# A decoder layer on one core: attention's filling passes as one sequence, and four output tiles begun early

## The chip, the cores and the metric

The kernel runs on 1 core of a Trainium2 chip. The metric is the device time of one execution in microseconds (us), as the median of several runs. Engines are named as in the profile: PE is the matrix engine (PEld its weight loads), DVE the vector engine, ACT the scalar engine, POOL the general engine, SP the engine that issues most DMAs.

## The reference, cut to what matters

One decoder layer over 1024 tokens of width 1024, in float32:

```python
h = rms_norm(x, norm_mix_pre)
q_d, k_d, v_d, u_p, q_m, gate_logits = split(h @ w_in)
a = diff_attention(q_d, k_d, v_d, lam)       # 8 heads, two softmax maps each, ALiBi, causal
a = rms_norm(a, subln_g) * (1 - lam_init)    # per head
y_attn = a @ w_attn_branch
y_pool = multiscale_pool(u_p, pool_w, pool_scale) @ w_pool_branch
y_mem  = memory_cross_attention(q_m, rms_norm(mem), w_mem_kv) @ w_mem_branch
gates = sigmoid(gate_logits)                 # three gates of width 1024
mix = gates[0]*y_attn + gates[1]*y_pool + gates[2]*y_mem
x = x + rms_norm(mix @ w_out, norm_mix_post)
h2 = rms_norm(x, norm_ffn_pre)
g, v = split(causal_depthwise_conv3(h2 @ w_up))
x = x + rms_norm((gelu(g) * v) @ w_down, norm_ffn_post)
```

## The kernel before, in words

Each float32 factor is kept as a high and a low part, and a product is three matrix passes (`mm3`, lines 103 to 105 of the profile). `split` (lines 89 and 90) makes the parts: ACT copies the high one, DVE subtracts for the low one. Products are made for 128 output channels by 512 tokens, over 8 blocks `k` of 128 input channels: 24 passes for such a half, 48 for both.

The parts of the layer run one after another: norms and the memory branch, the pooling branch, the two branches' gates and mix (`mixp_d`), values, keys and queries, attention, the merge of the attention branch, the output projection, the channel mixer. Many results are written to memory and read back.

Attention goes through 8 heads, each with 4 blocks `b` of two query tiles `u`. In a head, `scores` makes two maps of scores on PE (`pss`, line 1176), adds the bias and takes the extremum on DVE (`z`, line 1180), and takes exponentials on ACT (line 1185); `combine` joins the two maps on DVE (line 1199); `turn_weights` transposes them on PE (`pta`, line 1215) and splits them (`aT`); `weigh_values` multiplies by the values (`poa`, line 1232); `head_norm` sums squares on PE (`pn`, line 1250). The weights of a block are turned during the next block, so the last block of a head is finished in the first block of the next.

Between these stages `weave` puts filling: products that attention doesn't wait for at once. A generator is cut into steps by its `yield`s, and `steps(gen, n)` gives n closures that advance it. The filling of the kernel before is

- `head_keys(h + 1)` in heads 1 to 6: the keys of the next head but heads 0 and 1 (`pqk`), in 4 steps of 12 passes. Their weights were split earlier and lie in memory (`wk_d`). A half's result is split into `ktmp` and copied by four DMAs into the head's key tiles `ks` (line 1125). There are two sets of key tiles, for even and for odd heads;
- `gate(dt)`: the logits of gate 0 for 128 channels (`pg`), 8 steps of 6 passes. Its weights are loaded and split by `wsplit` at once. ACT copies a half out (`g`, line 1145), and POOL stores it to `gate_d`. Gates 0 and 1 were made ahead and wait in `g01` for their store;
- `values(h + 1)`: two loads of the next head's values, without passes.

Which head has which gate is a table:

```python
GATES = ((2, 3), (), (), (), (), (), (), (4,))
```

Weights of both kinds lie in the tags `wh` and `wl` of the pool `wst`, two buffers each; raw weights in `raw`, two buffers; `ktmp`, `g` and the tiles of the merge in the tag `t` of `gq`, two buffers. The banks of the matrix results are two of `b1`, two of `pj`, and two pairs of `b2`.

The order of instructions on each engine is not the order of the program text alone: a planner walks through the program with a model of times and lets an instruction go ahead of earlier ones that it takes to be not ready. So passes of gates can run before the place where they stand in the text. `issue_after` holds an instruction behind another one on its engine. On the chip each engine then runs its list in order.

Behind attention, gates 5 to 7 follow. Meanwhile the norms of heads 4 to 7 are finished (`head_norms(1)`, whose result `r_d` goes through memory), and each head's result `a` is loaded with its norm `rb`, scaled on DVE (line 1399) and split into `ath`, `atl`. The merge multiplies by `w_attn_branch` for 8 output tiles `dt` (`pya`): `merge_heads(dt, g)` does heads 0 to 3 (g = 0) or 4 to 7 (g = 1). Tiles 0 and 1 begin with heads 0 to 3 while heads 4 to 7 are not ready. `merge` loads the gate and `mixp_d` (`gm`, lines 1424 and 1425), takes the sigmoid on ACT (line 1426), multiplies and adds on DVE (lines 1427 and 1428) and splits into `mixh`, `mixl`. Then the output projection begins (`pout`).

Of the kernel before, what the change touches and what calls it, by code (L numbers as in the profile page):

```python
# [15 lines left out]
P = 128  # L16
# [6 lines left out]
NH = 8  # L23
# [18 lines left out]
def kernel(  # L42
# [1051 lines left out]
    def key_tiles(h):  # L1094
        return [qkp.tile([P, S], F32R, tag="ks%d%d" % (c, h % 2), name="ks%d" % c) for c in range(2)]
# [8 lines left out]

    def head_keys(h):


        wh, wl = [wst.tile([P, KT, P], F32R, tag=t, name=t) for t in ("wh", "wl")]
        with tc.issue_after(last["keys"].ins):
            for e, w in enumerate((wh, wl)):  # L1110
                nc.sync.dma_start(out=w.bitcast(F32), in_=wk_d[h, :, e])
        ks = key_tiles(h)
        for i in range(2):
            hs = slice(i * H, (i + 1) * H)
            pq = pbank(name="pqk")
            for k in range(KT):
                if k == H4:
                    yield
                mm3(pq, wh[:, k, :], wl[:, k, :], hTh[i][:, k, :], hTl[i][:, k, :], k == 0, k == KT - 1)
            tmp = gq.tile([P, 2, H], F32R, tag="t", name="ktmp")  # L1120
            split(tmp[:, 0, :], tmp[:, 1, :], pq)
            for c in range(2):
                for e in range(2):
                    r = 64 * (c ^ e)
                    nc.sync.dma_start(out=ks[c][r:r + 64, hs].bitcast(F32),
                                      in_=tmp[c * 64:c * 64 + 64, e, :].bitcast(F32))
            if i == 1:
                kts[h] = ks
            yield
# [170 lines left out]
    last["keys"] = last["load"]  # L1300
    with tc.issue_after(last["load"].ins):
        ready[3] = wsplit(chunk(w_in, C_G + 3 * P), [P, KT, P])
        for dt in range(2):
            nc.sync.dma_start(out=gate_d[dt], in_=g01[dt])
    GATES = ((2, 3), (), (), (), (), (), (), (4,))
    blocks = [(h, b) for h in range(NH) for b in range(4)]
    for h in range(NH):
# [34 lines left out]
        fillers = []  # L1342
        if h + 1 < NH:
            if h:
                fillers += steps(head_keys(h + 1), 4)
            for n, step in enumerate(steps(values(h + 1), 2)):
                fillers.insert(2 * n + 1, step)
        n = 0
        for dt in GATES[h]:
            for step in steps(first if dt == 2 else gate(dt), 6 if dt == 2 else 8):  # L1350
                fillers.insert(min(n, len(fillers)), step)
                n += 2
# [18 lines left out]
    def merge_heads(dt, g):  # L1371

        if g == 0:
            pys[dt] = wsplit(chunk(w_attn_branch, dt * P), [P, KT, P])[:2] + (bank(name="pya"), pbank(name="pya"))
        wh, wl, *py = pys[dt]
        for i in range(2):
            hs = slice(i * H, (i + 1) * H)
            for k in range(g * HG, (g + 1) * HG):
                mm3(py[i], wh[:, k, :], wl[:, k, :], ath[k][:, hs], atl[k][:, hs], k == 0, k == KT - 1)

    with tc.tile_pool(name="sub", reuse_waits="tile", bufs=4, side="right") as sub:
# [3 lines left out]
        for dt in range(5, KT):  # L1385
            for step in steps(gate(dt), 8):
                step()
        for h in range(NH):
            if h == HG:
                with tc.issue_after(ends["square"].ins):  # L1390
                    head_norms(1)

                for dt in range(2):
                    merge_heads(dt, 0)
# [23 lines left out]
    def merge(dt):  # L1418

        for i, py in enumerate(pys.pop(dt)[2:]):  # L1420
# [10 lines left out]
    for dt in range(KT):  # L1431
        if dt >= 2:
            merge_heads(dt, 0)
        merge_heads(dt, 1)
        merge(dt)
# [377 lines left out]
```

## Time and profile before

| what | value |
|---|---|
| median of 3 runs | 1727.56 us (1726.93 to 1729.04) |
| the profiled execution | 1727.11 us |
| its span, first to last instruction | 1725.3 us |
| granted clock of PE | 0.999 |
| head 0, heads 1 to 6, head 7 | 601.9, 638.3, 834.4 to 880.0 us of the span |
| gates behind attention | to 907.0 us |
| merge | 907.0 to 994.2 us |

A row of the timeline has the start, the time, the engine, the line, the operation, output and inputs, shapes, and in brackets the engine's idle time before it with what released it. A row of the table of waits has who waited for whom, the total, how often and the longest. A row by stretch has the stretch, its length, the busy time of each engine with its number of instructions, the granted clock, the share of the DMA engines and GB/s. The records of PE's passes overlap, and their ends are modelled.

### The profile page before, as it was taken

To read this page: it belongs to the slowest core of one execution; us is meant where nothing else is said; L and a number is where in the kernel's file an instruction comes from. 1 tells how busy PE (TensorE), PEld (TensorE's weight loads), DVE (VectorE), ACT (ScalarE), POOL (GpSimd) and SP (SyncE) were. 2 spreads that over 40 slices of the span, in tenths; PEclk is the share of its full clock that TensorE was granted. 3 is DMA by queue.
4 is the path that set the end of the run, shared out by engine and by line. 5 is a ranking of instruction groups with operands and counts; after the bars stand their busy time and mean duration, and the time that the engine had idled before them with its cause. 6 is when DMAs were issued, how large, how long until landed. Compare 5 with 4: busy or idle time off the path is not lost.

```text
span 1725.3 us, 22424 instructions
## 1 busy us (share of the span) xinstructions
PE 1711.3 (99%) x8106; PEld 1420.2 (82%) x8106; DVE 1242.2 (72%) x2059; ACT 888.5 (51%) x1585; POOL 45.0 (3%) x103
## 2 busy tenths in 40 slices
PE   9999999999999999999999999999999999999998
PEld 6888888888888888888888888888888888888886
DVE  7676876666666468888866555848888888877466
ACT  5434544444544467777744344645555555543453
POOL 0000000000000011111110000000000000000000
PEclk9999999999999999999999999999999999999999
DMA  8675544544874786665556571563433332583344
GB/s 275 242 254 220 161 152 155 161 136 158 260 229 147 210 226 183 175 181 152 136 206 223 194 217 41 173 224 92 129 119 95 122 100 84 195 305 99 108 144 144
DMA packets 232868, 294.41 MB, mean 171 GB/s; under 512 B 15930, under 2 KB 161591, under 8 KB 230071
## 3 DMA queue, kind: packets, MB, share of 16 engines
q1 hardware_dynamic: 229222, 285.61, 52.4%
q0 software_dynamic: 3520, 7.38, 1.2%
q8 instruction: 64, 1.05, 0.2%
q14 instruction: 46, 0.37, 0.1%
q10 hardware_dynamic: 16, 0.00, 0.0%
HBM read 201.10 MB, written 85.56 MB: 166 GB/s over the span
## 4 chain that ended last, share of the span: by engine, by line
PE 90%; DVE 5%; DMA 3%; ACT 1%; SPq 1%; issue 1%; DVEq 0%; ACTq 0%
PE pa L103 8%; PE pa L104 8%; PE pa L105 8%; PE pb L103 5%; PE pb L104 5%; PE pb L105 5%; PE pss L1176 3%; PE pd L103 2%; PE pd L105 2%; PE pd L104 2%; PE poa L1232 2%; PE pe L103 2%; PE pe L105 2%; PE pe L104 2%; PE pout L105 2%; PE pya L104 2%
## 5 line engine op out<-in xcount | busy, mean ns | idle before, releaser
L89 ACT ACTIVATE wpage<-s 128x512 fp32r<-128x512 f32 x136 | 85.2, 627 | 103.3 <-PE pb L105 33.6
L1580 DVE SCALAR_TENSOR_TENSOR cvt<-gv,cols,cvt 128x1023 f32<-128x1023 f32 x88 | 112.5, 1278 | 15.6 <-ACT cvt L1576 15.6
L90 DVE TENSOR_TENSOR wpage<-s,wpage 128x512 fp32r<-128x512 f32 x136 | 92.8, 688 | 40.1 <-ACT wpage L89 40.0
L1180 DVE CUSTOM_DVE_ANT_0 z<-pss,hbias 128x256 f32<-128x256 f32 (+7 forms) x128 | 94.5, 753 | 25.5 <-PE pss L1176 24.3
L1185 ACT ACTIVATE z<-z,mx 128x256 f32<-128x256 f32 (+7 forms) x128 | 98.8, 773 | 20.9 <-DVE mx L1180 20.8
L103 PE MATMUL pa<-T,wpage 128*128 128x512 f32 x264 | 102.9, 390 | 0.4 <-DVE gv L252 0.4
L104 PE MATMUL pa<-T,wpage 128*128 128x512 f32 x264 | 102.7, 389 | 0.0
L105 PE MATMUL pa<-T,wpage 128*128 128x512 f32 x264 | 102.7, 389 | 0.0
L1176 PE MATMUL pss<-ks,q 128*128 128x512 f32 (+5 forms) x384 | 86.6, 349 | 1.4 <-DVE mx L1180 1.4
L89 ACT ACTIVATE page<-blk 128x1024 fp32r<-128x1024 f32 (+1 forms) x42 | 41.4, 989 | 86.5 <-PE pe L104 50.6
L90 DVE TENSOR_TENSOR page<-blk,page 128x1024 fp32r<-128x1024 f32 (+1 forms) x42 | 47.6, 1133 | 40.6 <-ACT page L89 40.6
L1176 PEld LDWEIGHTS pss<-ks,q 128*128 128x128 f32 x384 | 62.9, 189 | 11.1 <-DVE mx L1180 6.2
L103 PE MATMUL pd<-page 128*128 128x512 f32 x176 | 68.7, 390 | 0.0
L104 PE MATMUL pd<-page 128*128 128x512 f32 x176 | 68.5, 389 | 0.0
L105 PE MATMUL pd<-page 128*128 128x512 f32 x176 | 68.3, 389 | 0.0
L103 PE MATMUL pa<-hT,wpage 128*128 128x512 f32 x168 | 65.4, 389 | 0.0
L104 PE MATMUL pa<-hT,wpage 128*128 128x512 f32 x168 | 65.4, 389 | 0.0
L105 PE MATMUL pa<-hT,wpage 128*128 128x512 f32 x168 | 65.4, 389 | 0.0
L1232 PEld LDWEIGHTS poa<-aT,v 128*128 128x128 f32 x480 | 60.8, 190 | 3.0 <-ACT srow L1252 1.4
L1232 PE MATMUL poa<-aT,v 128*128 128x256 f32 (+1 forms) x480 | 62.5, 280 | 0.0
L103 PEld LDWEIGHTS pa<-T,wpage 128*128 128x128 f32 x264 | 49.6, 188 | 11.4 <-DVE gv L252 0.8
L105 PEld LDWEIGHTS pa<-T,wpage 128*128 128x128 f32 x264 | 49.6, 188 | 10.5
(429 smaller groups left out, 4970.2 us busy)
## 6 DMA issues: line engine op xcount, KB each, us to landing
q<-q_d SPq DMA_DIRECT2D x64, 256.0 KB, 5.3
wd<-in_w_down_dram SPq DMA_DIRECT2D x22, 512.0 KB, 5.7
tw_d<-wd SPq DMA_DIRECT2D x11, 1024.0 KB, 4.0
rawv<-in_w_up_dram SPq DMA_DIRECT2D x22, 512.0 KB, 5.8
rawu<-in_w_up_dram SPq DMA_DIRECT2D x22, 512.0 KB, 3.9
ff_d<-cvt SPq DMA_DIRECT2D x22, 512.0 KB, 4.8
blk<-ff_d SPq DMA_DIRECT2D x20, 512.0 KB, 6.4
br<-tw_d SPq DMA_DIRECT2D x20, 512.0 KB, 4.1
```

What stands on the lines that cost most here:

```text
L89: copy = nc.scalar.activation(out=hi, in_=src, func=AF.Copy)
L90: nc.vector.tensor_tensor(out=lo, in0=src, in1=hi.bitcast(F32), op=ALU.subtract)
L103: nc.tensor.matmul(o, ah, bh, start=first, stop=False, skip_group_check=onto)
L104: nc.tensor.matmul(o, ah, bl, start=False, stop=False, skip_group_check=onto)
L105: return nc.tensor.matmul(o, al, bh, start=False, stop=last, skip_group_check=onto)
L1176: last["scores"] = nc.tensor.matmul(pss[:, i * H:i * H + m], q[:, j, c, ts], keys, start=(j == 0), stop=(j == 1))
L1180: nc.vector.tensor_tensor_reduce(out=halves(z[:, 0:n]), in0=pss.rearrange("p (a m) -> p a m", a=2)[:, 0:parts, 0:m], in1=halves(biases[h][ ...
L1185: nc.scalar.activation(out=z[:, 0:n], in_=z[:, 0:n], func=AF.Exp, scale=-1.0, bias=mx[:, c:c + 1], accum_out=sm if c else sums[:, h, t:t + 1])
L1232: nc.tensor.matmul(po[:, qs], (vh, vl)[i][:, k, :], w[j][:, ws], start=(n == 0), stop=(n == len(terms) - 1))
L1580: nc.vector.scalar_tensor_tensor(out=cv[:, sh:], in0=u[:, 0:S - sh], scalar=w, in1=cv[:, sh:], op0=ALU.mult, op1=ALU.add)
```

## The change

- One generator, `stream`, yields all filling in this order: gate 2, keys 2, gate 3, keys 3, 4, 5, 6, gate 4, keys 7, gate 5. Its 78 steps (6 left of gate 2, 8 for each of nine others) are dealt out to the 8 heads as evenly as whole steps allow: 10, 10, 9, 10, 10, 9, 10, 10. Keys are cut in 8 steps of 6 passes instead of 4 of 12.
- `fetch` loads the weights of the next item after the first step of the one before it (keys 2: ahead of head 0, in place of gate 3's weights). Gate 5 moves into attention, and gate 3 from head 0 to the second and third heads.
- The key tiles of a head are taken when its first half is done.
- Behind attention gates 6 and 7 remain. Four output tiles, not two, are begun with heads 0 to 3, head by head; tiles 2 and 3 take the paired banks.
- The branch's weights are loaded and split by half tiles, heads 0 to 3 and 4 to 7 apart (`merge_weights`), two of them in buffers of their own.
- Tiles 0 and 1 then take heads 4 and 5, then 6 and 7; tiles 2 to 7 follow one by one.

```diff
+    def fetch(kind, n):
+        if kind == "k":
+            ahead[n] = [wst.tile([P, KT, P], F32R, tag=t, name=t) for t in ("wh", "wl")]
+            with tc.issue_after(last["keys"].ins):
+                for e, w in enumerate(ahead[n]):
+                    nc.sync.dma_start(out=w.bitcast(F32), in_=wk_d[n, :, e])
+        else:
+            with tc.issue_after(last["load"].ins):
+                ready[n] = wsplit(chunk(w_in, C_G + n * P), [P, KT, P])
...
     def head_keys(h):
-        wh, wl = [wst.tile([P, KT, P], F32R, tag=t, name=t) for t in ("wh", "wl")]
-        with tc.issue_after(last["keys"].ins):
-            for e, w in enumerate((wh, wl)):
-                nc.sync.dma_start(out=w.bitcast(F32), in_=wk_d[h, :, e])
-        ks = key_tiles(h)
+        wh, wl = ahead.pop(h)
...
-                if k == H4:
+                if k in (2, 4, 6):
                     yield
...
+            if i == 0:
+                assert h - 2 not in kts
+                kts[h] = key_tiles(h)
...
+    fetch("k", 2)
     with tc.issue_after(last["load"].ins):
-        ready[3] = wsplit(chunk(w_in, C_G + 3 * P), [P, KT, P])
         for dt in range(2):
             nc.sync.dma_start(out=gate_d[dt], in_=g01[dt])
-    GATES = ((2, 3), (), (), (), (), (), (), (4,))
+    def stream():
+        items = [("g", 2), ("k", 2), ("g", 3), ("k", 3), ("k", 4), ("k", 5), ("k", 6), ("g", 4), ("k", 7), ("g", 5)]
+        for j, (kind, n) in enumerate(items):
+            gen = first if j == 0 else gate(n) if kind == "g" else head_keys(n)
+            for m, _ in enumerate(gen):
+                if m == 0 and 0 < j < len(items) - 1:
+                    fetch(*items[j + 1])
+                yield
+    fill = stream()
+    NF = 6 + 9 * 8
...
-        fillers = []
+        fillers = steps(fill, round(NF * (h + 1) / NH) - round(NF * h / NH))
         if h + 1 < NH:
-            if h:
-                fillers += steps(head_keys(h + 1), 4)
             for n, step in enumerate(steps(values(h + 1), 2)):
-                fillers.insert(2 * n + 1, step)
-        n = 0
-        for dt in GATES[h]:
-            for step in steps(first if dt == 2 else gate(dt), 6 if dt == 2 else 8):
-                fillers.insert(min(n, len(fillers)), step)
-                n += 2
+                fillers.insert(3 * n + 1, step)
...
+    def merge_weights(dt, g, own=None):
+        raw = wst.tile([P, HG, P], F32, tag="raw", name="rawm", bufs=2)
+        nc.sync.dma_start(out=raw, in_=w_attn_branch[g * HG * P:(g + 1) * HG * P, dt * P:(dt + 1) * P]
+                          .rearrange("(k p) c -> p k c", p=P))
+        if own:
+            w = own.tile([P, 2, HG, P], F32R, tag="page", name="mpage", bufs=2)
+        else:
+            w = wst.tile([P, 2, HG, P], F32R, tag=("wh", "wl")[pages[0] % 2], name="mpage")
+            pages[0] += 1
+        split(w[:, 0], w[:, 1], raw)
         if g == 0:
-            pys[dt] = wsplit(chunk(w_attn_branch, dt * P), [P, KT, P])[:2] + (bank(name="pya"), pbank(name="pya"))
...
+            if dt % 4 < 2:
+                pys[dt] = bank(name="pya"), pbank(name="pya")
+            else:
+                py = bank2(name="pya")
+                pys[dt] = py[:, 0:H], py[:, H:2 * H]
+        return w
...
-        for dt in range(5, KT):
+        for dt in range(6, KT):
             for step in steps(gate(dt), 8):
                 step()
+        ws = [merge_weights(dt, 0, sub) for dt in range(2)]
         for h in range(NH):
+            if h == 2:
+                ws += [merge_weights(dt, 0) for dt in range(2, 4)]
             if h == HG:
...
-                for dt in range(2):
-                    merge_heads(dt, 0)
+                for k in range(HG):
+                    for dt in range(4):
+                        merge_heads(dt, ws[dt], (k,))
...
-    for dt in range(KT):
-        if dt >= 2:
-            merge_heads(dt, 0)
-        merge_heads(dt, 1)
+    ws = [merge_weights(dt, 1) for dt in range(2)]
+    for ks in ((4, 5), (6, 7)):
+        for dt in range(2):
+            merge_heads(dt, ws[dt], ks)
+            if ks[0] == 6:
+                merge(dt)
+    for dt in range(2, KT):
+        for g in range(0 if dt >= 4 else 1, 2):
+            merge_heads(dt, merge_weights(dt, g), range(g * HG, (g + 1) * HG))
         merge(dt)
```

More of the change, by code (lines that the diff above doesn't have):

```diff
@@ L1103, in load_keys @@
                                                  in_=k_d[h, c * 64:c * 64 + 64, e])
-    def head_keys(h):
-        wh, wl = [wst.tile([P, KT, P], F32R, tag=t, name=t) for t in ("wh", "wl")]
-        with tc.issue_after(last["keys"].ins):
-            for e, w in enumerate((wh, wl)):
-                nc.sync.dma_start(out=w.bitcast(F32), in_=wk_d[h, :, e])
-        ks = key_tiles(h)
+    ahead = {}
+    def fetch(kind, n):
[7 more added lines that the diff above has]
+                ready[n] = wsplit(chunk(w_in, C_G + n * P), [P, KT, P])
+    def head_keys(h):
+        wh, wl = ahead.pop(h)
         for i in range(2):
@@ L1124, in head_keys @@
                     r = 64 * (c ^ e)
-                    nc.sync.dma_start(out=ks[c][r:r + 64, hs].bitcast(F32),
+                    nc.sync.dma_start(out=kts[h][c][r:r + 64, hs].bitcast(F32),
                                       in_=tmp[c * 64:c * 64 + 64, e, :].bitcast(F32))
-            if i == 1:
-                kts[h] = ks
             yield
@@ L1369, with merge_heads @@
     pys = {}
-    def merge_heads(dt, g):
-        if g == 0:
-            pys[dt] = wsplit(chunk(w_attn_branch, dt * P), [P, KT, P])[:2] + (bank(name="pya"), pbank(name="pya"))
-        wh, wl, *py = pys[dt]
+    def merge_weights(dt, g, own=None):
[8 more added lines that the diff above has]
+        split(w[:, 0], w[:, 1], raw)
+        if g == 0:
+            if dt % 4 < 2:
[4 more added lines that the diff above has]
+        return w
+    def merge_heads(dt, w, ks):
         for i in range(2):
             hs = slice(i * H, (i + 1) * H)
-            for k in range(g * HG, (g + 1) * HG):
-                mm3(py[i], wh[:, k, :], wl[:, k, :], ath[k][:, hs], atl[k][:, hs], k == 0, k == KT - 1)
+            for k in ks:
+                mm3(pys[dt][i], w[:, 0, k % HG, :], w[:, 1, k % HG, :], ath[k][:, hs], atl[k][:, hs],
+                    k == 0, k == NH - 1)
     with tc.tile_pool(name="sub", reuse_waits="tile", bufs=4, side="right") as sub:
@@ L1418, in merge @@
     def merge(dt):
-        for i, py in enumerate(pys.pop(dt)[2:]):
+        for i, py in enumerate(pys.pop(dt)):
             hs = slice(i * H, (i + 1) * H)
```

## The prediction

> **What bounds the kernel now.** I read the page first, then the busy time by stretch, then the waits of TensorE (PE), then the timeline around each of them, and last the waits of the SP queue and of the tail.
>
> ```profile
> span 1725.3 us, 22424 instructions
> PE 1711.3 (99%) x8106; PEld 1420.2 (82%) x8106; DVE 1242.2 (72%) x2059; ACT 888.5 (51%) x1585; POOL 45.0 (3%) x103
> ```
>
> PE is busy for all but 14 us of the span. The change removes no matrix pass, so it can win only idle time of PE, and only in the stretches that it touches. These are, in order: head 0, heads 1 to 6, head 7, the gates behind attention, the merge.
>
> ```profile
> core 0: us, PE busy (x) PEld busy (x) DVE busy (x) ACT busy (x) POOL busy (x), PEclk, DMA share, GB/s
> 601.90:638.30 36.40, 35.52 (x195) 30.47 (x194) 26.01 (x66) 23.10 (x55) 4.46 (x8) 1.00 0.85 223
> 638.30:834.40 196.10, 194.16 (x1202) 168.85 (x1201) 168.47 (x446) 147.90 (x364) 25.64 (x48) 1.00 0.64 175
> 834.40:880.00 45.60, 44.79 (x270) 37.74 (x270) 35.07 (x83) 32.23 (x77) 6.98 (x13) 1.00 0.35 95
> 880.00:907.00 27.00, 27.00 (x120) 22.35 (x120) 16.01 (x27) 9.30 (x13) 3.21 (x6) 1.00 0.86 309
> 907.00:994.20 87.20, 87.20 (x385) 71.99 (x384) 50.65 (x62) 35.62 (x48) 0.54 (x1) 1.00 0.62 208
> ```
>
> The idle time of PE is 0.88 us in head 0, 1.94 in heads 1 to 6 and 0.81 in head 7: 3.63 us. Behind attention it is nothing. So the whole prize lies in attention; behind it the change can only lose. The granted clock is 1.00 everywhere.
>
> What PE waits for there, and where six of the nine waits stand:
>
> ```profile
> PE pss L1176 <- DVE mx L1180: 1.4, 4, 0.5
> PE pta L1215 <- DVE z L1199: 1.2, 3, 0.6
> PE pg L103 <- ACT g L1145: 0.6, 1, 0.6
> PE pg L103 <- ACT wh L89: 0.2, 1, 0.2
> 602.72 0.74 PE L1176 MATMUL pss<-ks,q 128*128 128x256 f32 x4 [0.29 <-DVE mx L1180]
> 672.13 0.99 PE L1215 MATMUL pta<-ident,z 128*128 128x128 f32 x7 [0.56 <-DVE z L1199]
> 705.91 0.50 PE L1176 MATMUL pss<-ks,q 128*128 128x256 f32 x2 [0.28 <-DVE mx L1180]
> 770.63 0.40 PE L103 MATMUL pqk<-hTh,wh 128*128 128x512 f32 x1
> 770.86 0.40 PE L104 MATMUL pqk<-hTl,wh 128*128 128x512 f32 x1
> 771.62 0.50 PE L1176 MATMUL pss<-ks,q 128*128 128x256 f32 x2 [0.36 <-DVE mx L1180]
> 836.67 0.50 PE L1176 MATMUL pss<-ks,q 128*128 128x256 f32 x2 [0.51 <-DVE mx L1180]
> 838.85 0.50 PE L103 MATMUL pg<-hTh,wh 128*128 128x512 f32 x1 [0.17 <-ACT wh L89]
> ```
>
> The starts at 770.63 and 770.86 show the pitch of a 512-column pass: 0.23 us, though its record is 0.40 long. The third pass should have come at 771.09 and came at 771.62: 0.53 us lost where the row shows 0.36. So each wait costs about 0.17 us more than its row. Nine waits with 3.4 us in the rows are 3.4 + 9 x 0.17 = 5.0 us; with the small remainder up to 3.63, **the ceiling of the gain is 5.2 us**.
>
> [...]
>
> **The change part by part.**
>
> *The even sequence.* Filling is now 78 steps of 6 passes (2 by 3), 6 left of gate 2 and 8 each for six key heads and gates 3, 4, 5: 468 passes, 10 or 9 steps a head. Before, head 0 had 84 passes, heads 1 to 6 had 48 each in steps of 12, head 7 had 48. A pass costs 0.227 us (the merge's row: 87.20 us for 384 recorded passes of the output tiles and one more). So heads 1 to 6 get 9.75 x 6 - 48 = 10.5 more passes, 2.4 us each; head 0 loses 24 to 26, about 5.7 us. PE per inner head goes from 196.1 / 6 = 32.7 to 35.1 us, while DVE stays at 168.47 / 6 = 28.1 and ACT at 24.7: DVE's share falls from 86% to 80%. Head 0 goes from 36.4 to about 30.7 us, against DVE's 26.0 less one weight split: about 81 to 85%. No engine but PE can become the bound of a head; only local waits count.
>
> The waits of the inner heads all stand at a head's start, where scores are 128 or 256 columns wide and PE needs the last block's weights of the head before:
>
> ```profile
> 799.72 1.15 ACT L1185 ACTIVATE z<-z,mx 128x1024 f32<-128x1024 f32 x1 [0.64 <-DVE mx L1180]
> 801.26 1.28 DVE L1199 SCALAR_TENSOR_TENSOR z<-z,mx 128x1024 f32<-128x1024 f32 x1
> 802.60 0.98 PE L1215 MATMUL pta<-ident,z 128*128 128x128 f32 x7 [0.35 <-DVE z L1199]
> 803.89 0.40 PE L103 MATMUL pqk<-hTh,wh 128*128 128x512 f32 x1
> ```
>
> Exponential, combination and turn stand in a chain, and the turns were put before passes of filling that came 1.3 us later. The order is planned ahead, so a stall here is the planner's error of some tenths of a microsecond, not a lack of filling. More filling, in finer steps, puts PE further behind DVE when it reaches these places: 2.4 us a head against waits of 0.28 to 0.56. But the planner can again put the turns right at the time it believes they are ready. I can't read which from this trace. The bounds: all five waits of the starts of heads 2 to 6 go (all of the 1.2 us under turns, two of the four under scores, 0.3 and 0.4, is 1.9, plus 5 x 0.17: 2.7 us), or none does. I take 1.7, above the middle because the slack added is several times each wait.
>
> *Head 7.* The waits at 836.67 and 838.85 (0.51 + 0.17, plus 2 x 0.17: 1.0 us) come where gate 4's weights were split too late to fill. Now key 7's last two steps and gate 5 stand there, and gate 5's weights are fetched one whole item earlier. I take 1.0; the bounds are 0 and 1.0.
>
> *Head 0.* The 0.59 us wait on the gate's eviction comes behind the split of gate 3's weights on ScalarE:
>
> ```profile
> 620.15 1.04 ACT L89 ACTIVATE wh<-raw 128x1024 fp32r<-128x1024 f32 x1
> 621.09 0.57 ACT L1145 ACTIVATE g<-pg 128x512 f32<-128x512 f32 x1
> 621.72 0.50 PE L103 MATMUL pg<-hTh,wh 128*128 128x512 f32 x1 [0.59 <-ACT g L1145]
> gate_d<-g SPq DMA_DIRECT2D x2, 512.0 KB, 10.3
> ```
>
> The next item is now key 2, whose weights come split from memory, so this split is out of the way. Against it, 1 MB for key 2 takes the place of 0.5 MB ahead of the two stores of gates 0 and 1, and the eviction needs one of their two buffers. At 223 GB/s (head 0's row) 0.5 MB more is 2.3 us. Bounds: 0.76 us won, or up to 2.3 lost; I take 0.4 won, since fewer filling passes are asked for early and the second half pass of gate 2 is later too.
>
> *Fetching.* Gates 3, 4 and 5 put three weight splits (1.04 us ACT, about 1.2 DVE each) into attention's middle instead of its ends. They may stand ahead of an exponential; DVE has 7 us of slack a head. Bounds 0 and 3 x 0.59 (the one such wait seen) = 1.8; I take 0.1.
>
> *Behind attention.* 119 passes of gates ran after 880 (the row's 120, less one of a head's norm), then 48 of the two begun tiles: 167 x 0.227 = 37.9 us, until 917.9. Then all of heads 4 to 7 were wanted within 2.7 us:
>
> ```profile
> L104 PE MATMUL pya<-atl,wh x128: 389/389/504, 907.2 to 993.8; 128*128 128x512 f32 x128
> L90 DVE TENSOR_TENSOR atl<-a,ath x8: 1221/1226/1227, 892.5 to 918.9; 128x1024 fp32r<-128x1024 f32 x8
> ```
>
> Head 7 was ready at 918.9 + 1.2 = 920.1, and was wanted at 917.9 + 9 x 0.227 = 919.9: the cover was used up to the last. Now two gates and four tiles are 192 passes, 43.6 us, less what is pulled into attention: 25 passes before (192 of gates 4 to 7, less 48 and 119), now 25 or, as head 7 has 12 more of its own, 13: 37.9 to 40.6 again, but heads 4 and 5 of two tiles come first (24 passes, 5.4 us), so heads 6 and 7 have 5 us more. No wait arises, and none goes: 0. All eight banks hold tiles then; the first to be reused is tile 0's, 5 x 12 = 60 passes, 13.6 us, after its last pass, which covers its eviction.
>
> *The pages.* Sixteen half pages replace eight whole ones: ACT 16 x 0.627 instead of 8 x 1.06 (10.0 for 8.5 us), DVE 16 x 0.688 instead of 8 x 1.22 (11.0 for 9.8), and eight more loads on SP.
>
> ```profile
> L89 ACT ACTIVATE wpage<-s 128x512 fp32r<-128x512 f32 x136 | 85.2, 627 | 103.3 <-PE pb L105 33.6
> L90 DVE TENSOR_TENSOR wpage<-s,wpage 128x512 fp32r<-128x512 f32 x136 | 92.8, 688 | 40.1 <-ACT wpage L89 40.0
> L89 ACT ACTIVATE wh<-raw 128x1024 fp32r<-128x1024 f32 x9 | 9.5, 1059 | 6.5 <-PE pg L104 4.6 <-PE pya L104 1.9
> L90 DVE TENSOR_TENSOR wl<-raw,wh 128x1024 fp32r<-128x1024 f32 x9 | 11.0, 1220 | 0.8 <-ACT wh L89 0.8
> SPq L1424 <- DVE mixl L90: 35.6, 11, 6.9
> raw<-in_w_attn_branch_dram SPq DMA_DIRECT2D x6, 512.0 KB, 4.4
> ```
>
> The merge keeps DVE and ACT at 50.65 and 35.62 of 87.2 us, so 1.2 and 1.5 us more are covered. A page's load can stand on SP behind a gate load that waits up to 6.9 us; with 4.4 to land and 1.3 to split it is ready 12.6 us after its turn. Four page buffers at 24 passes (5.4 us) each give some 16 to 21 us. I take 0.
>
> **The sum:** 1.7 + 1.0 + 0.4 - 0.1 = 3.0 us. The profiled execution took 1727.1 us around its span of 1725.3; that is 0.45 below the median of 1727.56. Forecast for the median: 1727.6 - 3.0 = 1724.6; I round it to 1724.5. Its own range is 1722.5 to 1726.5.
>
> **The rivals.**
>
> *Nearly all waits go:* 4.6 to 5.2 us, since PE lags DVE everywhere; 1722.7. For it: the waits are tenths, the slack added is microseconds. Against it: PE still waits at 602.72, before any filling can help.
>
> *The waits stay.* Four of nine are for a score bank, of which there are two, and the change adds none; the turns come at the same planned instant. Then only head 7's 1.0 us goes and small new ones come: 1727.0. [...]
>
> *Slower: a key half behind a waiting query load.* Key 3's last step now falls into head 3, and its four copies into the key tiles go over SP, which waits long for query buffers:
>
> ```profile
> SPq L1091 <- PE pss L1176: 32.5, 5, 15.4
> ks<-ktmp SPq DMA_DIRECT2D x48, 128.0 KB, 4.1
> ```
>
> Behind a wait of 15.4 us and 4.1 to land, the half would come 19.5 us into the head, and the third block wants it about a third in, 12 us by estimate: 7.5 us of stall, which decides from the point where the copies are queued after a query load that waits for the head's end. 1727.6 + 7.5 - 3.0 = 1732. Against it: the query load of that half of the head is issued after its second block, well behind the first step.
>
> *That it does nothing at all* is the second rival, less head 7.
>
> **How the numbers follow.** Chances: the forecast 0.42, nearly all waits go 0.25, waits stay 0.17, slower (the queue, or the late stores in head 0, or a late page) 0.16. The time is the first's. A change of 0.2%, 3.45 us, is about what can be told from none, so the bound of faster is 1724.1: the second case, and a third of the first, 0.39; same 0.45; slower 0.16. The range takes all of the first three and most small losses: 1721.0 to 1729.5.
>
> **What would show it.** Right: PE idle from 600 to 890 falls from 3.6 to about 1.5 us, the two waits at head 7's start and the one on the gate's eviction are gone, attention ends some 8 to 11 us later, and PE from there to the end of the merge has no wait. Wrong: waits of turns and scores at each head's start as long as before; a PE wait above 1 us on a key tile, a page or a head's weights; an ACT split ahead of an exponential that PE then waits for.

## The result, and the profile after

The changed kernel takes 1733.81 us (median of 6 runs, 1733.00 to 1738.46) against 1727.49 us before (6 runs, 1726.54 to 1729.04): ratio of the means 1.0040, 95% interval 1.0027 to 1.0053. Each later run is compared with executions of the kernel before beside it, whose medians lie between 1726.63 and 1727.68 us; its ratio and interval stand behind its median. The prediction said 1724.5 us, and its range ended at 1729.5. The change made the kernel slower by 6.3 us.

The page of the changed kernel, its span and its engines:

```profile
span 1732.2 us, 22457 instructions
PE 1714.0 (99%) x8106; PEld 1420.8 (82%) x8106; DVE 1245.0 (72%) x2067; ACT 889.3 (51%) x1593; POOL 45.2 (3%) x103
```

PE's instructions are as many as before. The busy time by stretch: attention with the gates behind it (from the first scores to the first pass of an output tile), the merge, and the output projection (from its first pass to its last); then the output projection before. Columns as in the prediction: stretch, its length, busy time and count of PE, PEld, DVE, ACT and POOL, granted clock, DMA share, GB/s. The row for attention before comes further down.

```profile
602.65:909.42 306.77, 302.44 (x1784) 259.90 (x1782) 241.52 (x616) 210.90 (x506) 40.43 (x75) 1.00 0.62 168
909.40:996.40 87.00, 87.00 (x385) 72.05 (x384) 56.52 (x72) 37.19 (x54) 0.54 (x1) 1.00 0.70 237
996.40:1093.00 96.60, 93.21 (x433) 76.74 (x433) 52.57 (x100) 39.02 (x75) 0.00 (x0) 1.00 0.40 127
```

```profile
994.20:1086.50 92.30, 92.30 (x433) 76.87 (x432) 51.35 (x98) 37.72 (x73) 0.00 (x0) 1.00 0.39 120
```

The merge has no idle time of PE, as forecast. The loss stands just behind it: the output projection, which the change doesn't touch, takes 96.6 us where it took 92.3, and PE is idle in it for 3.4 us where its row before shows no idle time. Attention should have been 3 us shorter than the 305.1 us of before and was 1.6 longer in this execution. What PE waits for, from attention to the first passes of the output projection:

```profile
PE pout L104 <- DVE wol L90: 2.7, 2, 1.6
PE pta L1224 <- DVE aT L90: 1.5, 4, 0.7
PE pss L1185 <- DVE mx L1189: 1.1, 2, 0.8
PE pta L1224 <- DVE z L1208: 1.1, 4, 0.4
PE pout L103 <- ACT woh L89: 0.7, 1, 0.7
...
```

The first and the fifth row are new: PE waits for the split weights of the output projection (`woh` and `wol`, made by `load_wo` from `w_out`). Neither the prediction's sum nor its rivals name these tiles. The timelines of PE, ScalarE, VectorE and SP at that place show who was late. Columns: start, duration, what it is, and in brackets the idle time before it with what ended it.

```profile
1002.74 0.49 PE L103 MATMUL pout<-woh,mixh 128*128 128x512 f32 x1 [0.68 <-ACT woh L89]
1004.86 0.50 PE L104 MATMUL pout<-wol,mixh 128*128 128x512 f32 x1 [1.62 <-DVE wol L90]
1007.62 0.50 PE L104 MATMUL pout<-wol,mixh 128*128 128x512 f32 x1 [1.09 <-DVE wol L90]
```

```profile
991.61 1.06 ACT L89 ACTIVATE woh<-rawo 128x1024 fp32r<-128x1024 f32 x1 [2.54 <-DMA rawo<-in_w_out_dram]
...
999.74 0.63 ACT L1460 ACTIVATE gm<-gm 128x512 f32<-128x512 f32 x1 [6.03 <-issue]
...
1001.65 2.94 ACT L89 ACTIVATE woh<-rawo 128x1024 fp32r<-128x1024 f32 x3
```

```profile
993.85 1.29 DVE L90 TENSOR_TENSOR mixl<-gm,mixh 128x512 fp32r<-128x512 f32 x2
...
1006.35 3.49 DVE L90 TENSOR_TENSOR wol<-rawo,woh 128x1024 fp32r<-128x1024 f32 x3
```

```profile
975.11 0.33 SPq L1447 DMA_DIRECT2D rawo<-in_w_out_dram  x1
...
984.76 9.53 SPq L1447 DMA_DIRECT2D rawo<-in_w_out_dram  x5
994.56 0.33 SPq L1458 DMA_DIRECT2D gm<-gate_d  x1
...
995.47 0.37 SPq L1458 DMA_DIRECT2D gm<-gate_d  x1
```

Read it from the end. PE's third wait is for the splits that VectorE starts at 1006.35. They stand behind the last tile's eviction, which begins with the sigmoid at 999.74: ScalarE had been idle for 6.03 us ahead of it, with the weights of the output projection behind it in its order. The row names no releaser (`issue`), but that sigmoid needs the last tile's gate rows, which SP asked for at 994.56 and 995.47; 5.2 us from load to sigmoid is also what the last half took before (988.24 to 993.43). And these rows are written into a buffer that is free when the subtraction into `mixl` at 993.85, the end of the tile before, is through. SP itself is free of the five weight loads only at 994.29, about as late, so this trace alone doesn't tell the queue from the buffer. Before, the first weight load and the same two gate loads went out at 964.42, 985.52 and 988.24:

```profile
964.42 0.33 SPq L1413 DMA_DIRECT2D rawo<-in_w_out_dram  x1
...
985.52 0.33 SPq L1424 DMA_DIRECT2D gm<-gate_d  x1
...
988.24 0.32 SPq L1424 DMA_DIRECT2D gm<-gate_d  x1
```

The output projection begins at 994.2 before and at 996.46 after: the last gate loads went out 8.7 and 6.0 us ahead of it, and now 1.9 and 1.0 us ahead. The first load of the output projection's weights, 29.8 us ahead of it before, goes out 21.4 us ahead of it now (975.11).

### The profile page after: what moved, and what is told of

Its sections match the earlier page's. It is cut to its first block, busy times and chain, and to the rows that moved or that the text cites. A ratio compares the mean times of both kernels' runs of the same rounds, so it can differ in the third digit from the quotient of the medians.

```text
span 1732.2 us, 22457 instructions
## 1 busy us (share of the span) xinstructions
PE 1714.0 (99%) x8106; PEld 1420.8 (82%) x8106; DVE 1245.0 (72%) x2067; ACT 889.3 (51%) x1593; POOL 45.2 (3%) x103
## 4 chain that ended last, share of the span: by engine, by line
PE 87%; DVE 5%; DMA 4%; ACT 2%; issue 1%; SPq 0%; DVEq 0%; ACTq 0%
PE pa L103 8%; PE pa L105 8%; PE pa L104 8%; PE pb L103 5%; PE pb L104 5%; PE pb L105 5%; PE pss L1185 3%; PE pd L105 2%; PE pd L104 2%; PE pd L103 2%; PE poa L1241 2%; PE pe L105 2%; PE pe L104 2%; PE pe L103 2%; PE pta L1224 2%; PE pout L104 2%
```

## The experiments

**Which half of the change costs it.** One kernel has attention of before and the new merge (the parts of the diff from `merge_weights` on, with gates 5, 6 and 7 behind attention). Of the code the lines that matter are shown, with `...` for those between them:

```
+    def merge_weights(dt, g, own=None):
...
+                for k in range(HG):
+                    for dt in range(4):
+                        merge_heads(dt, ws[dt], (k,))
...
+    for ks in ((4, 5), (6, 7)):
+        for dt in range(2):
+            merge_heads(dt, ws[dt], ks)
...
```

> The merge of the changed kernel (four tiles begun, half pages) behind the attention of the kernel before; gates 5 to 7 stay behind attention. Theory M, the loss is the late weights of the output projection: 1727.5 + 4 = 1731.5 us, with 3 to 3.5 us of PE waits on the projection's weights (pout) and the waits of attention as before (3.4 us). Rival A, the loss lies in attention's filling: 1727.5 us and no wait at pout.

1730.97 us (10 runs), ratio 1.0021 [1.0012, 1.0031]. The other has the even sequence, with gate 5 still behind attention, and the merge of before:

```
+        items = [("g", 2), ("k", 2), ("g", 3), ("k", 3), ("k", 4), ("k", 5), ("k", 6), ("g", 4), ("k", 7)]
...
+    NF = 6 + 9 * 8
```

> The even sequence without gate 5 in front of the merge of the kernel before (whole weights, two tiles begun, gates 5 to 7 behind attention). Theory M: no wait at pout; the start of the output tiles comes some 1.6 us later than before, as in the changed kernel, with waits at the turns: 1729 us. Rival A: 1733. The forecast on record (waits of attention go): 1724.5.

1732.77 us (8 runs), ratio 1.0030 [1.0020, 1.0040]. What PE waits for with the new merge alone, and its output projection's row:

```profile
PE pout L104 <- DVE wol L90: 2.7, 2, 1.6
PE pss L1176 <- DVE mx L1180: 1.4, 4, 0.5
PE pta L1215 <- DVE z L1199: 1.3, 3, 0.6
PE pout L103 <- ACT woh L89: 0.7, 1, 0.7
```

```profile
994.20:1090.80 96.60, 93.15 (x433) 76.73 (x432) 52.62 (x100) 38.99 (x75) 0.00 (x0) 1.00 0.39 124
```

The two new rows are there in the same size with attention unchanged, so the new merge makes them by itself. This run came out as theory M said, in time too. The even sequence alone has no such wait; what it loses is in attention, which takes 309.4 us there. Its time lies at rival A's number, but it is no clean half of the change: its list has 70 steps and is dealt out as if it had 78, so the last head is left with almost no filling. PE's waits in that head come to 2.4 us by their rows, against 0.4 in the changed kernel's last head.

**Half pages against whole pages.** Tiles 4 to 7 take their weights whole, as before:

```
-    for dt in range(2, KT):
-        for g in range(0 if dt >= 4 else 1, 2):
-            merge_heads(dt, merge_weights(dt, g), range(g * HG, (g + 1) * HG))
...
+    for dt in range(4, KT):
+        wh, wl, _ = wsplit(chunk(w_attn_branch, dt * P), [P, KT, P])
...
+                mm3(pys[dt][i], wh[:, k, :], wl[:, k, :], ath[k][:, hs], atl[k][:, hs], k == 0, k == NH - 1)
```

> The changed kernel, but tiles 4 to 7 of the merge load and split whole weights again, so that four loads, not eight, take the raw buffers ahead of the projection's weights. Theory M2, the raw buffers are held too long: the projection's loads start some 10 us earlier and the waits at pout (3.4 us in the rows, 4.3 of time) go: 1729.5 us. Theory M1, the order on SP (five of the projection's loads stand ahead of the last tile's gate loads and each waits for a buffer): that order is the same here, so most of the waits stay: 1732 to 1733.8.

1730.12 us (11 runs), ratio 1.0012 [1.0003, 1.0022]; the output projection takes 95.8 us. The waits on `wol` are 2.7 us as before, the one on `woh` is gone. Whole pages give 0.8 us of the 4.3 back. So the waits stay, as theory M1 said, though the time is near theory M2's number: the median falls by some 4 us, to 2.4 us above the kernel before beside it. Attention, in which the two kernels are the same, took 304.9 us in this profile where it took 306.8 in the changed kernel's. And none of the 11 executions has a mean granted clock below 0.999, where half of the changed kernel's have 0.997 (last section). That the pages brought either isn't shown.

**The order on SP.** The merge's gate and mixture loads issued by POOL instead of SP:

```
-            nc.sync.dma_start(out=g, in_=gate_d[dt][:, hs])
-            nc.sync.dma_start(out=mp, in_=mixp_d[dt][:, hs])
+            nc.gpsimd.dma_start(out=g, in_=gate_d[dt][:, hs])
+            nc.gpsimd.dma_start(out=mp, in_=mixp_d[dt][:, hs])
```

> The changed kernel, but the merge's loads of gates and partial mix are issued by POOL instead of SP. Theory M1 (the last tile's gate loads wait on SP behind the projection's loads, ScalarE waits for them, and the projection's splits stand behind that sigmoid): the waits at pout go, 1729.5 us. Theory M2 (raw buffers): the projection's weights are as late as before, 1733 or more.

1749.44 us (4 runs), ratio 1.0128 [1.0114, 1.0142]. The move made a new loss (the merge takes 96.2 us instead of 87.0), so it says nothing of SP's order. The cleaner trial leaves the loads on SP and puts the last four loads of the output projection's weights behind the last tile's gate loads, once in the changed kernel and once in the kernel with the new merge alone; the changed kernel ran again beside them:

```
-        nc.sync.dma_start(out=raw, in_=w_out[k * P:(k + 1) * P, :])
+        with tc.issue_after(marks["gm"].ins) if k >= 4 else nullcontext():
+            nc.sync.dma_start(out=raw, in_=w_out[k * P:(k + 1) * P, :])
...
-            nc.sync.dma_start(out=mp, in_=mixp_d[dt][:, hs])
+            marks["gm"] = nc.sync.dma_start(out=mp, in_=mixp_d[dt][:, hs])
```

> The changed kernel, but the last four loads of the projection's weights are issued on SP behind the last tile's gate loads. Theory M1 (the order on SP): the last sigmoid comes some 6 to 8 us earlier, the waits at pout fall from 3.4 to under 0.5 us, and the time is 4 us below the changed kernel. Theory M2 (raw buffers held by half pages): the projection's weights are as late or later, the waits stay at 3.4 or grow.

> The new merge behind the attention of before, with the same order on SP. Theory M1: nothing is left of the loss, 1727 to 1728 us, equal to the kernel before. Theory M2: 1731 as without it. That the half pages cost something else in the merge: between the two, with the wait at another place.

> The changed kernel itself, to have it beside the others on one chip. Its attention took 306.8 us from the first scores to the first output pass; two kernels with the same instructions up to there took 304.9 and 305.2, and two with the attention of before 305.1 and 304.9. If the difference is chance, this run has 305 to 307 and the time is 1732 to 1734; the waits at pout (3.4 us) stay in either case.

1732.85 us, ratio 1.0034 [1.0021, 1.0047]; 1731.26 us, 1.0025 [1.0016, 1.0034]; and the changed kernel 1733.62 us, 1.0035 [1.0022, 1.0047]. In the changed kernel with this order the last gate loads went out ahead of four of the five weight loads and were late all the same (992.6 and 993.5 us, for an output projection that began at 994.8), and PE waited 3.3 us. What SP waited for from 984 to 995 us shows why:

```profile
SPq L1459 <- DVE mixl L90: 6.0, 1, 6.0
```

The theory of SP's order fell: at the head of the queue, the gate load waits 6.0 us for its buffer, until the last subtraction of an earlier half.

**An early split in attention.** The split of a gate's weights put five steps behind their load:

```
-                ready[n] = wsplit(chunk(w_in, C_G + n * P), [P, KT, P])
+                late_raw[n] = wload(chunk(w_in, C_G + n * P), [P, KT, P])
...
+                if m == 5 and j + 1 < len(items) and items[j + 1][0] == "g":
+                    dt = items[j + 1][1]
+                    ready[dt] = wsplit(None, [P, KT, P], late_raw.pop(dt))
```

> The changed kernel, but gate weights fetched inside attention are split five steps after their load, not at once. In the profile of the changed kernel ScalarE waits 1.07 us for gate 5's weights and PE 0.84 us behind it. Theory F (the early split stands on ScalarE and waits for its load): that pair of waits is gone and attention from the first scores to the first output pass takes 304.5 to 305 us. Rival (chance of that execution, or the turns): 305 to 307 as before. Waits at pout unchanged.

1734.45 us (5 runs), ratio 1.0042 [1.0030, 1.0055]; attention 305.4 us, in the rival's range. But the trial doesn't settle its question. Here are the places in the changed kernel where ScalarE waits for fetched weights inside the heads (gate 4's, then gate 5's), and PE's wait behind each:

```profile
768.53 1.06 ACT L89 ACTIVATE wh<-raw 128x1024 fp32r<-128x1024 f32 x1 [0.95 <-DMA raw<-in_w_in_dram]
770.86 0.55 PE L1224 MATMUL pta<-ident,z 128*128 128x128 f32 x3 [0.70 <-DVE aT L90]
833.61 1.06 ACT L89 ACTIVATE wh<-raw 128x1024 fp32r<-128x1024 f32 x1 [1.07 <-DMA raw<-in_w_in_dram]
837.33 1.97 PE L1185 MATMUL pss<-ks,q 128*128 128x512 f32 x7 [0.84 <-DVE mx L1189]
```

In the trial the loads go out at 760.21 and 824.68 us (760.73 and 825.09 in the changed kernel), and the splits, at 768.05 and 832.05, stand between the same instructions in ScalarE's list as in the changed kernel. The text was moved, the list was not. The first split still waits 0.71 us for its load, the second doesn't wait. Nor does the median speak of attention: four of the five executions have a mean granted clock of 0.996 or 0.997, and the output projection took 99.2 us in the profile.

What speaks is the spread between the eight profiled executions that have the changed kernel's list. PE has neither of the two waits in two of them (the kernel with whole pages, the one with four gate buffers), and there attention takes 304.9 us. In the other six these waits come to between 0.36 and 1.54 us and attention takes 305.2 to 306.8; the longest go together, as in the profile above. So weights that land too late for their split cost attention up to 1.9 us. That is read from the traces; no run took these waits away.

**Gate buffers or raw buffers.** Now two theories were left for the output projection's late weights: the two buffers for gate rows, which each half of a tile holds from its load to its last subtraction, or the two raw buffers, which the half pages share with the weights of the output projection. Four kernels tell them apart. Gate buffers:

```
+    gmx = dstack.enter_context(tc.tile_pool(name="gmx", reuse_waits="tile", bufs=2, side="right"))
...
-            gm2 = gq.tile([P, 2, H], F32, tag="t", name="gm2")
+            gm2 = (gmx if i else gq).tile([P, 2, H], F32, tag="t", name="gm2")
```

Raw buffers (3 of their own in one kernel, 1 in the kernel with both):

```
+    rxp = dstack.enter_context(tc.tile_pool(name="rx", reuse_waits="tile", bufs=3, side="right"))
...
+        raw = rxp.tile([P, D], F32, tag="ro", name="rawo") if k < 3 else \
+            wst.tile([P, D], F32, tag={6: "wh", 7: "wl"}.get(k, "raw"), name="rawo", bufs=2)
```

The new merge alone, with four gate buffers:

> The kernel with attention of before and the new merge (1730.97 and 92.27 + 4.3 us between the first and the last pass of the output projection), in which the buffer for the second half of each tile's gate rows comes from a pool of its own with two buffers, so that four are in use where there were two. Theory G (two gate buffers): the passes of tiles 0 to 3 end 2.7, 5.4 and 5.4 us apart instead of 10.9, each half holds one of two buffers for about 8 us from its load to its last subtraction, so evictions fall behind, the splits and loads of the output projection's weights stand behind them in ScalarE's, VectorE's and SyncE's order, and PE waits at the start of the output projection. With four buffers the waits on woh and wol (3.5 us) go below 1 us, time about 1727. Theory R (raw buffers): the twelve half pages hold the two raw buffers, which the weights of the output projection need; nothing changes, waits 3.5 us, about 1731.

1727.28 us (11 runs), ratio 1.0004 [0.9995, 1.0012]. The changed kernel with four gate buffers:

> The changed kernel with the same two added gate buffers. Theory G: waits at the start of the output projection below 1 us, about 1728 to 1730. Theory R: as the changed kernel, 1733 to 1734, waits of 3.4 us.

1728.51 us (11 runs), ratio 1.0014 [1.0005, 1.0023]. With three raw buffers instead:

> The changed kernel, in which the first three loads of the output projection's weights go into three raw buffers of their own instead of the two that they share with the merge's half pages. Theory R: those loads land before the last three tiles, waits at the start of the output projection below 1 us, about 1728 to 1730. Theory G: the evictions of the last tiles are as late as before, and the last gate loads with them; waits fall by 1 us at most, about 1733.

1731.33 us (9 runs), ratio 1.0027 [1.0017, 1.0037]. With both:

> The changed kernel with both: two more gate buffers, and a raw buffer of its own for the first load of the output projection's weights. Theory G: as with the gate buffers alone, 1728 to 1730. Theory R: better than with the gate buffers alone by what one raw buffer brings, 1 to 2 us. Both theories in part: this one is lowest, and no PE wait is left at the start of the output projection; by attention's time in earlier runs (304.9 to 306.8 us against 305.1) it ends within 1 us of before.

1729.11 us (11 runs), ratio 1.0012 [1.0003, 1.0021], no better than the gate buffers alone. The output projection of the new merge alone with four gate buffers, of the changed kernel with them, and of the changed kernel with three raw buffers, and the wait that is left in the last:

```profile
994.90:1087.20 92.30, 92.30 (x433) 76.90 (x432) 52.55 (x100) 37.83 (x73) 0.00 (x0) 1.00 0.39 119
```

```profile
994.70:1087.00 92.30, 92.30 (x432) 76.86 (x431) 52.56 (x100) 37.82 (x73) 0.00 (x0) 1.00 0.39 120
```

```profile
995.50:1090.80 95.30, 92.92 (x433) 76.66 (x432) 52.63 (x100) 39.00 (x75) 0.00 (x0) 1.00 0.39 122
```

```profile
PE pout L104 <- DVE wol L90: 2.4, 2, 1.4
```

With four gate buffers the output projection is back at 92.3 us and PE has no wait in it, in both kernels; with more raw buffers 3.0 of 4.3 us stay. There the first of the weight loads, with a buffer of its own, goes out at 976.75, 18.7 us ahead of the output projection and no earlier than without it (21.4). In SP's timeline of the changed kernel with four gate buffers the last gate loads now come far ahead of its start at 994.7:

```profile
973.48 0.32 SPq L1459 DMA_DIRECT2D gm<-gate_d  x1
...
979.23 0.33 SPq L1459 DMA_DIRECT2D gm<-gate_d  x1
...
980.15 9.97 SPq L1448 DMA_DIRECT2D rawo<-in_w_out_dram  x5
```

They go out 21.2 and 15.5 us ahead of it instead of 1.9 and 1.0, while the five weight loads on SP still take as long (9.97 for 9.53 us). The control is the kernel before with the same four buffers:

> The kernel before with the same four gate buffers, a control. It has no wait at the start of the output projection, so theory G (two gate buffers hold up the new merge alone) expects no change, 1727 within 0.1%, and 92.3 us between the first and the last pass of the output projection. If the buffers bring something of their own, it is faster by over 1 us, and what they bring to the changed kernel is not all cure of its merge.

1727.81 us (11 runs), ratio 1.0003 [0.9995, 1.0012]. The buffers bring nothing by themselves; they only take away what the new merge had added. The new order on SP that comes with them is not enough alone: with two buffers the gate loads ahead of the weight loads were late too. With four, the changed kernel is still 1.9 us above the 1726.63 of the kernel before beside it.

**Where attention's gain went.** With four gate buffers the changed kernel's attention takes as long as the one before, in an execution that has no wait behind fetched weights. Two more trials ask whether the waits at the turns can be taken away. Twice as long steps of filling, half as many:

```
+    def pairs(g):
+        for _ in g:
+            next(g, None)
+            yield
-    fill = stream()
-    NF = 6 + 9 * 8
+    fill = pairs(stream())
+    NF = 3 + 9 * 4
```

> The changed kernel with four gate buffers (1728.51; attention 304.87 us in its profile against 305.13 before, where the prediction expected 3 us less), in which the filling goes in with twice as long steps, twelve passes where there were six, half as many. Theory L (length of a step): six passes (1.4 us) behind a turned tile are too few to cover the split that gives its bank back, so PE waits at the turns (2.3 us in the profile against 1.4 before); with twelve (2.8 us) these waits fall below 1.4 us and attention takes 303.5 or less, time about 1727. Theory S (sum of the work): attention's heads have next to no idle time to give, waits move from the scores to the turns and back; attention stays within 0.7 us of 304.9, and the waits on scores rise by what those at the turns fall.

1728.14 us (11 runs), ratio 1.0005 [0.9996, 1.0014]. The turn of a block's later weights as a stage of its own, behind the block's second scores:

```
...
-                    turn_weights(*blocks[n - 1])
+                    turn_weights(*blocks[n - 1], False)
                 stages.append(weights)
             stages.append(lambda h=h, b=b: scores(h, b, 1))
+            if n >= 1:
+                stages.append(lambda n=n: turn_weights(*blocks[n - 1], True))
```

> The changed kernel with four gate buffers, in which the turn of a block's third and fourth group of weights is a stage of its own behind the block's second scores, so that filling and scores come between the second and the third group. Theory B (two turn banks): the waits for the low half of an earlier group (0.9 us, 3 times) go, and attention takes about 304. Theory S: they go and others of the same size come, attention within 0.7 us of 304.9, about 1728.5.

1728.45 us (11 runs), ratio 1.0005 [0.9996, 1.0014]. Attention's rows, in this order: before; the changed kernel with four gate buffers; the same with long steps; the same with the turns apart:

```profile
601.87:907.00 305.13, 301.50 (x1783) 259.43 (x1782) 245.56 (x620) 212.56 (x507) 40.28 (x75) 1.00 0.64 181
```

```profile
602.24:907.11 304.87, 302.06 (x1783) 259.88 (x1782) 240.71 (x615) 209.98 (x505) 40.27 (x75) 1.00 0.62 169
```

```profile
603.67:909.39 305.72, 302.53 (x1783) 260.98 (x1782) 242.93 (x617) 212.71 (x507) 40.44 (x75) 1.00 0.61 169
```

```profile
601.88:907.41 305.53, 302.33 (x1784) 261.09 (x1783) 242.60 (x616) 211.03 (x506) 40.44 (x75) 1.00 0.62 168
```

The waits of PE up to the first passes of the merge (910 us), first of the changed kernel with four gate buffers, then with long steps:

```profile
PE pta L1224 <- DVE z L1208: 1.1, 4, 0.4
PE pta L1224 <- DVE aT L90: 0.9, 3, 0.5
PE pss L1185 <- DVE mx L1189: 0.3, 1, 0.3
PE pya L103 <- ACT g L1154: 0.2, 1, 0.2
PE pta L1224 <- ACT sq L1247: 0.2, 1, 0.2
```

```profile
PE pss L1185 <- DVE mx L1189: 1.4, 4, 0.5
PE pta L1224 <- ACT sq L1247: 0.7, 3, 0.3
PE pta L1224 <- DVE aT L90: 0.5, 1, 0.5
```

Three orders of the same work wait in three ways. The even sequence has its waits at the turns (2.2 us) and few at the scores (0.3); long steps give 1.2 at the turns and 1.4 at the scores. With the turns apart 0.7 are left at the turns and 1.1 stand at the scores, and the sum of PE's idle time, 3.2 us by its row (305.53 less 302.33), equals the second's. The waits were exchanged, as theory S expected. The third order's attention is within its 0.7 us of 304.87, the second's is 0.85 above, outside it; neither is shorter. No version beats the kernel before.

## Why the prediction was wrong

*The step that failed* is "Behind attention ... No wait arises, and none goes: 0", and with it "The pages ... I take 0". The prediction followed PE's passes to the end of the merge and stopped there. Inside the merge it was right: no idle time. But a tile of the merge isn't done with its last pass. Its eviction holds a gate buffer until the last subtraction, and the weights of the output projection come behind it on ScalarE, VectorE and SP. The prediction gave these loads and splits no term, and counted cover only for banks ("13.6 us ... covers its eviction") and for page buffers. The runs showed 4.3 us there, which two more gate buffers take away.

*The row was there.* The prediction quoted the gate loads' wait for `mixl` (35.6 us, 11 times, longest 6.9), but read it only as a delay for a page queued behind. It says more: before the change, gate loads already stood still for their two buffers. What the change does to them follows from the order of the passes. Before, tiles 0 to 3 ended about 5.4 us (0 to 1) and 10.9 us apart; now tiles 0 and 1 end 2.7 us apart, and 2 and 3 follow at 5.4 us each. From there on both kernels end a tile every 10.9 us. Measured from the start of the output projection backwards, the merge's product on VectorE (line 1427 before) for tile 3's second half comes at 43.2 us before and at 33.9 us after, 9.3 us later. Tile 6's second half, whose end frees the last buffer, comes at 8.8 us before and at 6.4 after, its first half at 12.7 and 7.0. In between the lag had shrunk (tile 5's second half: 21.5 and 18.4); it grows again where the splits of the output projection's weights, themselves late, stand ahead of tile 6's eviction on ScalarE and VectorE and wait for their loads. That two gate buffers are too few for the new spacing is shown by the two added ones, which take all 4.3 us away, in two kernels. The way from there to PE is read from the timelines.

*What the whole 6.3 us are.* The output projection's 4.3 us (96.6 less 92.3) are settled. Attention was to give 3.0 us and gave nothing: without waits behind fetched weights the new list takes as long as the old one, with them longer. The list of before took 304.9 to 305.1 us in the five profiled executions that have it (1 of before, 4 with it behind another merge or other buffers). The new list took 304.9 to 306.8 us, 305.6 in the mean, in the eight that have it: 0.7 us more, an estimate from these. That leaves about 1.3 us. Some executions lose 3 us more in the output projection (last section). By its mean granted clock of 0.997 that may be half of the changed kernel's: six of twelve in its two sets of runs, 1735.2 us in the mean against 1733.3 for the others. This can make up most of the rest; it wasn't measured apart.

*The starts of heads 2 to 6, 1.7 us.* The row behind it went as forecast: waits on scores fall from 1.4 us to 0.3 (with four gate buffers). But the turns rise from 1.2 to 2.2 us. The prediction had named this ("the planner can again put the turns right at the time it believes they are ready") and chose against it by the size of the slack. The runs are nearest to the rival "the waits stay", whose small new waits came too: slack of microseconds a head did not help a chain of exponential, combination and turn whose place in the order moved with the filling. Nor is idle time by the records a measure of the gain: it falls from 3.63 to 2.81 us in the second row above, and the stretch is shorter by only 0.26, since PE's busy time rises by 0.56 for the same passes. Why it rises isn't shown.

*Head 7, 1.0 us, and head 0, 0.4 us.* Right in what goes: no row for the gate's eviction or for a gate's weights (`PE pg`) is left in the changed kernel's waits. It shows in no sum: waits at other places came for them, among them one of 0.84 us behind gate 5's weights and, in some executions, 0.2 to 0.4 us for a gate's eviction at the merge's first passes. *The last norm* comes at 893.1 us after 879.8, 13 us later where 8 to 11 were forecast.

*Splits in attention's middle, 0.1 us.* This term was mis-sized. PE's waits behind the fetched weights are 1.54 us in the profile after and 0.6 in the mean of the eight executions, and the 0.7 us by which the new list is longer go with them. They are of the kind that the prediction's last sign of being wrong had named, a split on ScalarE that PE then waits behind; here it stands ahead of a turn's copy and of the scores' bias.

*The slower rival* (a key half behind a waiting query load) didn't happen: no PE wait on a copy into the key tiles is in the changed kernel's rows (one of 0.4 us is in those of the trial with the turns apart). The kernel became slower by another way, one queue and one buffer further on than any rival looked.

*The score banks.* They are two before and after, and the rival "the waits stay" rested on that. The waits on scores fell from 1.4 to 0.3 us with the same two banks (in the kernel with four gate buffers). Too few buffers did cost time at another place, the gate rows, where two more took 4.3 us away; what showed it was a DMA queue's wait (6.0 us on SP, with the later weight loads), not a gap of PE that repeats.

## What to carry to other kernels

When tiles are reordered so that several finish close together, follow each one past its last matrix pass: how long does its eviction hold its buffers, how many are there, and what stands behind it on the same engines, down to the weights of the next stage. A queue that waits long for a buffer in the old profile (here SP, 35.6 us for the gate rows) points to a buffer that sets when its loads go out: the last gate loads went out 8.7 and 6.0 us ahead of the next stage before, and 1.9 and 1.0 us ahead after. Here that cost nothing while the spacing stayed, and 4.3 us at the next stage's start when it changed. And idle time made of many waits of tenths of a microsecond was not a prize that more filling collected: with four gate buffers it fell in attention from 3.63 to 2.81 us, and the length only from 305.13 to 304.87. Count what a reordering has gained by the length of the stretch, not by the rows that vanish. Where a planner orders the instructions, look in the trace whether a trial moved them at all, before reading anything from its time.

## What was not expected of the hardware

The same three waits at the start of the output projection cost more in some executions. In another execution of the changed kernel PE's granted clock fell to half behind the second of them. By stretches of 2 us, first that execution, then the one of the profile after:

```profile
1004.00:1006.00 2.00, 0.38 (x2) 0.27 (x2) 1.68 (x2) 2.00 (x4) 0.00 (x0) 1.00 0.06 23
1006.00:1008.00 2.00, 1.63 (x6) 0.78 (x5) 1.99 (x3) 1.45 (x2) 0.00 (x0) 0.74 0.51 136
...
1010.00:1012.00 2.00, 2.00 (x6) 1.59 (x5) 1.91 (x3) 0.72 (x2) 0.00 (x0) 0.50 0.92 265
```

```profile
1004.00:1006.00 2.00, 1.14 (x5) 0.95 (x6) 1.67 (x3) 2.00 (x4) 0.00 (x0) 1.00 0.07 11
...
1010.00:1012.00 2.00, 2.00 (x10) 1.67 (x9) 1.04 (x2) 0.25 (x2) 0.00 (x0) 1.00 1.13 311
```

In the first, passes start 0.43 us apart from 1009.08 to 1013.35, in the second 0.23; the output projection takes 99.6 us there and 96.6 here. The waits are 3.8 and 3.4 us in all, each at most 1.6 us long. They are not quite alike: the first one is 1.29 us there and 0.68 here, so that from 1001.94 to 1005.73 PE starts one pass in 3.8 us there, and here one in 3.2 (1001.67 to 1004.86). In the first execution the granted clock is 1.00 in the rows of the first two waits, 0.74 in the row behind the second, then 0.50; in the second execution it is 1.00 throughout. What made the difference, the length of the waits, their place or something else, isn't shown: no run here varies one of them alone.
